# Attention logits of two query blocks made together, the low part of q against the high part of k in two row halves of the array

## The chip, the cores and the metric

The kernel runs on one core of a Trainium2 chip. The metric is the device time of one execution in microseconds (us); the time before is the median of three runs. The profile is of one further execution of the same program.

## What is computed

The reference is a two-layer encoder trunk over 2048 frames of 1024 features. Layer 0 mixes by causal pooling, layer 1 by stick-breaking attention over 16 heads of 64 features. Around them stand projections, norms and gates. The part that matters here is the attention:

```python
logits = jnp.einsum('bhtd,bhsd->bhts', q[:, :, t0:L], k[:, :, :L]).astype(jnp.float32) * SB_SCALE
...
log_keep = jnp.where(mask, jax.nn.log_sigmoid(-logits), 0.0)
later = lax.cumsum(log_keep, axis=log_keep.ndim - 1, reverse=True) - log_keep
log_a = jax.nn.log_sigmoid(logits) + later
a = jnp.where(mask, jnp.exp(log_a), 0.0)
outs.append(jnp.einsum('bhts,bhsd->bhtd', a.astype(v.dtype), v[:, :, :L]))
```

All of it is asked for in float32. The kernel multiplies in the type float32r and carries each operand as a high part and a low part, the low one being what rounding left over; a product is then a sum of several matmuls of parts.

## The kernel before, in words

**Tiling.** The sequence is cut into four chunks of 512 frames (`W5`), and each chunk into four blocks of 128. Features lie on the 128 partitions. The dense layers of a chunk are written as a generator, `stream()`, which yields after each matmul. They compute q, k and v per chunk and write the parts of q and k to memory outside the core as `qd` and `kd`: for each head two layers (high, low) of 64 features by 512 frames.

**Attention.** The list `slots` holds one entry per query chunk, head and key chunk: 160 in all, namely 16 heads times 1, 2, 3 and 4 key chunks. Each slot has four steps, one for each block `j` of 128 queries. In the slot where key chunk and query chunk are the same (`diag`), block `j` needs only the first `(j + 1) * 128` keys, so its width is 128, 256, 384 or 512; in all other slots it is 512. A step does, in the order in which it is written out:

- `turn` (L750) transposes pieces of the finished weights of five steps ago (`LAG_T`) through TensorE into a `psa` bank; ScalarE copies the high part out (L758), VectorE takes the low part (L760, written later in the step).
- at `j == 0`, `begin(i + 1)` (L799) issues the loads of the next slot: `load_k` (L711), and for a new head `load_q` (L704). At `j == 3`, `begin_v` (L810) loads v.
- `front` (L730) makes the logits of block `j` in a `psl` bank with two matmuls, and a sigmoid by ScalarE (L739) takes them out to a tile `pp`.
- the scan of the step before (L743, VectorE) multiplies along the keys.
- `fill` (L844) takes about half of the step's share of dense matmuls (`psd` banks) from the stream.
- `gather` (L762) multiplies transposed weights of seven steps ago (`LAG_G`) by v into a `pso` bank, and `fill` follows again.

**Order.** While attention runs, `state["hold"]` is set, and TensorE's instructions keep the order in which the program writes them (L46 and L50 are the two helpers through which all go). Loads of q, k, v and dense weights (`wpair`, L156) are all issued on the queue of SyncE (SP), one after the other. There are eight PSUM banks, two for each of the tags `psl`, `psa`, `pso` and `psd`.

**The operands of the logits.** For a head, `kk` holds 128 partitions: the high part of k on 0 to 63 and the low part on 64 to 127. `qa` holds the high part of q above the low part, `qb` the same with the halves exchanged. The first matmul sums high by high and low by low over the 128 partitions, the second low by high and high by low. Two buffers serve `kk` (L103), four serve `qa` and `qb` together (L105). At the very beginning, `load_first` (L342) borrows buffers of these tags for the first eight tiles of the input.

Of the kernel before, what the change touches and what calls it, by code (L numbers as in the profile page):

```python
# [9 lines left out]
F32 = mybir.dt.float32  # L10
F32R = mybir.dt.float32r
# [4 lines left out]
P = 128  # L16
# [4 lines left out]
HD = 64  # L21
W5 = 512
# [9 lines left out]
def f(ap):  # L32
    return ap.bitcast(F32)
# [3 lines left out]
def trunk_kernel(ctx, tc, x, p, a_norm, wu_t, wz_a, w_group, a_scale, a_w_out, kv_norm, w_kv,  # L37
                 k_norm, b_norm, b_w_q, b_w_z, b_q_norm, b_w_out, ple_a, ple_b, gate_a, gate_b, out):
    nc = tc.nc
# [15 lines left out]
    cp = ctx.enter_context(tc.tile_pool(name="cp", bufs=1))  # L55
# [19 lines left out]
    g_s, g_b, g_kv = (gains[:, i * KT : (i + 1) * KT] for i in range(3))  # L75
    gqk = cp.tile([P, 1], F32, name="gqk")
    gs = cp.tile([P, 2], F32, name="gs")
    halo = [[cp.tile([P, HALO], F32, name=f"halo{o}_{i}") for i in range(2)] for o in range(KT)]
    for o in range(KT):
        V.memset(halo[o][0], 0.0)  # L80

    def scratch(name, shape):
        return dram.tile(shape, F32, name=name)
# [4 lines left out]
    qd = [[scratch(f"qd{s}_{h}", [2, HD, W5]) for h in range(NH)] for s in range(NSUB)]  # L88
    kd = [[scratch(f"kd{s}_{h}", [2, HD, W5]) for h in range(NH)] for s in range(NSUB)]
# [3 lines left out]
    pool = ctx.enter_context(tc.tile_pool(name="pool", bufs=2))  # L93
    psum = ctx.enter_context(tc.tile_pool(name="psum", bufs=2, space=bass.MemoryType.PSUM))

    def flat(tag, bufs, dt=F32):
        return lambda nm, dt=dt: pool.tile([P, W5], dt, tag=tag, name=nm, bufs=bufs)
# [4 lines left out]
    row = flat("row", 6)  # L102
    keyt = flat("kk", 2, F32R)  # L103
    valt = flat("vv", 3, F32R)
    qryt = flat("q", 4, F32R)  # L105
    ppt = flat("pp", 9)
    pair = lambda nm: pool.tile([P, 2, W5], F32R, tag="act", name=nm, bufs=16)
    t4 = lambda nm: pool.tile([P, 2, W5], F32R, tag="t4", name=nm, bufs=3)
# [2 lines left out]
    def bank(tag, nm):  # L111
        return psum.tile([P, W5], F32, tag=tag, name=nm)
# [227 lines left out]
    first_x = []  # L340

    def load_first():  # L342
        for o in range(KT):
            xin = (qryt, ppt, keyt, valt)[(0, 2, 0, 3, 0, 2, 0, 3)[o]]("xin", F32)
            (nc.sync, nc.scalar)[o % 2].dma_start(out=xin, in_=x[o * P : (o + 1) * P, 0:W5])
            first_x.append(xin)

# [354 lines left out]


    def load_q(c, h):  # L704
        qa, qb = qryt("qa"), qryt("qb")
        nc.sync.dma_start(out=f(qa), in_=qd[c][h].rearrange("l d n -> (l d) n"))
        for l in range(2):
            nc.sync.dma_start(out=f(qb)[(1 - l) * HD : (2 - l) * HD], in_=qd[c][h][l])
        return qa, qb

    def load_k(kc, h):  # L711
        kk = keyt("kk")
        nc.sync.dma_start(out=f(kk), in_=kd[kc][h].rearrange("l d n -> (l d) n"))
        return kk

    def load_v(kc, h):
        vv = valt("vv").rearrange("q (k n) -> q k n", k=4)
# [3 lines left out]
    def load_ends(c, b):  # L721
        en = pool.tile([P, 4, 4], F32, tag="en", name="en")
        for j in range(4):
            nc.sync.dma_start(out=en[:, :, j], in_=ve[c][b][j].rearrange("(m q) -> q m", q=P))
        return en

    last = {}
    ends = {}

    def front(st, j):  # L730
        w = (j + 1) * P if st["diag"] else W5
        r0 = W5 - w
        ps = bank("psl", "psl")
        qs = slice(j * P, (j + 1) * P)
        (qa, qb), kk = st["q"], st["k"]
        T.matmul(ps[:, :w], qa[:, qs], kk[:, :w], start=True, stop=False)
        T.matmul(ps[:, :w], qb[:, qs], kk[:, :w], start=False, stop=True)
        pp = ppt("pp")
        A.activation(out=pp[:, r0:], in_=ps[:, :w], func=AF.Sigmoid, scale=-1.0)  # L739

        def scan():
            least = floor[:, r0:][:, ::-1] if st["diag"] else floor[:, 0:1].to_broadcast([P, w])
            V.tensor_tensor_scan(out=pp[:, r0:][:, ::-1], data0=pp[:, r0:][:, ::-1], data1=least,  # L743
                                 initial=1.0 if st["diag"] else st["carry"][j], op0=ALU.mult, op1=ALU.max)
            st["carry"][j] = pp[:, r0 : r0 + 1]
            st["a"].append((pp, r0))

        return scan

    def turn(st, kt):  # L750
        j0 = kt if st["diag"] else 0
        pt = bank("psa", "psa")
        for j in range(j0, 4):
            pp, r0 = st["a"][j]
            T.transpose(pt[:, j * P : (j + 1) * P], pp[:, r0 + kt * P : r0 + (kt + 1) * P], ident)
        at = att("at")
        cs = slice(j0 * P, W5)
        A.copy(out=at[:, 0, cs], in_=pt[:, cs])  # L758
        st["at"][kt] = at
        return lambda: V.tensor_tensor(out=at[:, 1, cs], in0=pt[:, cs], in1=f(at[:, 0, cs]), op=ALU.subtract)  # L760

    def gather(st, kt):  # L762
        cs = slice((kt if st["diag"] else 0) * P, W5)
        if st["diag"] and kt == 0:
            st["o"].append(bank("pso", "pso"))
        po, at, vv = st["o"][0], st["at"].pop(kt), st["v"]
        T.matmul(po[:, cs], vv[:, kt, :], at[:, 0, cs], start=(st["diag"] and kt == 0), stop=False)
        T.matmul(po[:, cs], vv[:, kt, :], at[:, 1, cs], start=False, stop=(st["last"] and kt == 3))
        if st["last"] and kt == 3:
            half, os, c, h2 = st["h"] % 2, st["os"], st["c"], st["h"] // 2  # L770
            mine, other = slice(half * HD, (half + 1) * HD), slice((1 - half) * HD, (2 - half) * HD)
            A.copy(out=os[mine], in_=po[other])
            V.tensor_tensor(out=os[mine], in0=po[mine], in1=os[mine], op=ALU.add)  # L773
            if half:
                gated(c, h2, os)
# [16 lines left out]
    active, head = {}, {}  # L792
    run = stream()

    def until(mark):
        while mark not in marks:
            next(run)

    def begin(i):  # L799
        c, h, kc = slots[i]  # L800
        until((c, h // 8))
        if kc == c:
            if h % 8 == 0:
                ends[c, h // 8] = load_ends(c, h // 8)
            os = head["os"] if h % 2 else pool.tile([P, W5], F32, tag="os", name="os", bufs=2)
            head.clear()
            head.update(q=load_q(c, h), carry=[None] * 4, o=[], os=os)
        active[i] = dict(head, c=c, h=h, k=load_k(kc, h), diag=kc == c, last=kc == 0, a=[], at={})

    def begin_v(i):  # L810
        c, h, kc = slots[i]
        active[i]["v"] = load_v(kc, h)

    def rate(i):
        c = slots[min(i, len(slots) - 1)][0]
        parts = 66 + (0, 0, -8, 8)[c]
        return (parts * 24.0) / (64 * (c + 1) - (5 if c < NSUB - 1 else 0))

    nc.scalar.dma_start(out=g_a, in_=a_norm)
    pump()  # L820
    fold_load(3)
    load_first()
    wq["by"] = nc.sync
    wq["cap"] = UNITS
# [10 lines left out]
    until((0, 0))  # L835
    state["solo"], state["hold"] = False, True
    begin(0)
    begin_v(0)
    for _ in range(60):
# [4 lines left out]
    def fill(share):  # L844
        nonlocal owed, count
        owed += share
        while owed >= 1.0:
            next(run, None)
            owed -= 1.0
            count += 1  # L850
            if count % 36 == 0 and kept and (1, 0) in marks:
                keep(*kept.pop(0))

    scan = None
    for n in range(4 * len(slots) + LAG_G):
        i, j = divmod(n, 4)
        x_ = rate(i)
        i2, j2 = divmod(n - LAG_T, 4)
        low = turn(active[i2], j2) if 0 <= i2 < len(slots) else None
        due, scan = scan, None  # L860
        if i < len(slots):
            if j == 0 and i + 1 < len(slots):
                begin(i + 1)
            if j == 3 and i + 1 < len(slots):
                begin_v(i + 1)
            scan = front(active[i], j)
        if due:
            due()
        if low:
            low()  # L870
        fill(x_ / 2)
        i3, j3 = divmod(n - LAG_G, 4)
        if 0 <= i3 < len(slots):
            gather(active[i3], j3)
            if j3 == 3:
                active.pop(i3)
        fill(x_ / 2)
# [69 lines left out]
```

## Time and profile before

| | |
|---|---|
| time, median of 3 runs | 2834.18 us (2833.43 to 2836.98) |
| time of the profiled execution | 2834.65 us |
| its span, first to last instruction | 2832.9 us |
| matmuls | 13400 |
| of these for logits (`psl`) | 1280 |
| bytes moved by DMA | 643.37 MB |
| mean granted clock of TensorE | 0.985 |

The span is nearly all of the time. Lines of the profile name an engine (PE is TensorE's matmuls, PEld its weight loads, DVE is VectorE, ACT ScalarE, POOL GpSimd, SP SyncE and SPq its DMA queue), the source line, the operation, the tiles as out<-in, and the shape. In a group the count follows an x, then come the busy time, the mean duration of one in ns, and the idle time ahead of it with what ended it. In a timeline the first number is the start in us from the beginning of the span, the second the time until the last of the merged instructions ends. In the table by stages, the first number after the bounds is the length, followed by the busy time and count of each engine, the granted clock, the share of the DMA engines and GB/s.

### The profile page before, as it was taken

How to read it: one execution, taken by the hardware profiler on the slowest of the kernel's cores; microseconds unless marked ns; L12 is line 12 of the kernel's file. 1: busy time of each engine (PE TensorE's matmuls, PEld its weight loads, DVE VectorE, ACT ScalarE, POOL GpSimd, SP SyncE). 2: the span in 40 equal slices, each digit the busy share in tenths (PEclk: the TensorE clock that was granted, in tenths of full speed). 3: DMA queues.
4: the chain of work that ended last, by engine and by line, in shares of the span. 5: the costliest groups of instructions: out<-in, count | busy, mean ns of one | idle time of the engine just before them, and what ended most of it. 6: DMA issues, size and time to landing. Idle time of an engine off the chain costs nothing.

```text
span 2832.9 us, 38130 instructions
## 1 busy us (share of the span) xinstructions
PE 2733.4 (96%) x13400; PEld 2246.7 (79%) x13400; DVE 1840.4 (65%) x2369; ACT 1271.2 (45%) x2496; POOL 870.4 (31%) x699
## 2 busy tenths in 40 slices
PE   7999979999988999999999999999999999999999
PEld 7888857878866787788778888888888888888777
DVE  5645444655334686766458888776777877777872
ACT  4435542344433445545344456554454444444441
POOL 1354422455423354553213434221211101111002
PEclk8999989999999999999999999999999999999999
DMA  5647899556788966786776444778577667656535
GB/s 213 222 142 278 309 323 307 178 176 208 257 258 282 334 224 218 235 308 228 244 251 219 146 147 153 241 225 274 177 230 240 244 213 255 207 198 230 176 127 185
DMA packets 306123, 643.37 MB, mean 227 GB/s; under 512 B 48646, under 2 KB 81414, under 8 KB 305932
## 3 DMA queue, kind: packets, MB, share of 16 engines
q1 hardware_dynamic: 304348, 639.62, 68.1%
q8 instruction: 105, 1.72, 0.3%
q10 hardware_dynamic: 1584, 1.33, 0.1%
q14 instruction: 86, 0.70, 0.1%
HBM read 471.43 MB, written 161.02 MB: 223 GB/s over the span
## 4 chain that ended last, share of the span: by engine, by line
PE 79%; DMA 8%; DVE 5%; SPq 2%; issue 2%; ACT 2%; POOL 2%; ACTq 0%; DVEq 0%; POOLq 0%
PE psd L46 55%; PE psl L46 8%; PE pso L46 7%; PE psa L50 7%; DMA wpair<-once 3%; DVE pp L743 2%; DVE at L760 1%; DMA wraw<-in_b_w_q_dram 1%; PE pst L50 1%; DMA xin<-in_x_dram 1%; DMA vs<-vr 1%; POOL wpair L144 1%; PE pst L46 1%; SPq L523 1%; DMA kraw<-in_b_w_out_dram 1%
## 5 line engine op out<-in xcount | busy, mean ns | idle before, releaser
L743 DVE TENSOR_TENSOR_SCAN pp<-pp,floor 128x512 f32<-128x512 f32 (+3 forms) x640 | 774.7, 1210 | 34.5 <-ACT pp L739 33.6
L760 DVE TENSOR_TENSOR at<-psa,at 128x512 fp32r<-128x512 f32 (+3 forms) x640 | 387.1, 605 | 431.9 <-ACT at L758 429.6
L46 PE MATMUL psd<-wpair,x 128*128 128x512 f32 x2304 | 620.5, 403 | 38.8 <-DMA wpair<-once 22.7
L758 ACT CAST at<-psa 128x512 fp32r<-128x512 f32 (+3 forms) x640 | 333.6, 521 | 690.6 <-PE psa L50 665.4
L46 PE MATMUL psd<-x,wpair 128*128 128x512 f32 x2304 | 599.3, 393 | 3.5 <-ACT sg L481 3.5
L46 PEld LDWEIGHTS psd<-wpair,x 128*128 128x128 f32 x2304 | 426.0, 191 | 139.6 <-DMA wpair<-once 38.0
L46 PEld LDWEIGHTS psd<-x,wpair 128*128 128x128 f32 x2304 | 427.0, 188 | 92.5 <-ACT sg L481 4.6
L46 PE MATMUL psd<-xp,wpair 128*128 128x512 f32 x1536 | 391.8, 396 | 6.4 <-DMA wpair<-once 6.4
L50 PE MATMUL psa<-ident,pp 128*128 128x128 f32 x2176 | 347.2, 274 | 17.4 <-DVE pp L743 6.6
L46 PE MATMUL pso<-at,vv 128*128 128x512 f32 (+3 forms) x1280 | 361.5, 364 | 0.2 <-DVE at L760 0.2
L50 PEld LDWEIGHTS psa<-ident,pp 128*128 128x128 f32 x2176 | 274.8, 141 | 104.8 <-DVE at L760 12.2
L739 ACT ACTIVATE pp<-psl 128x512 f32<-128x512 f32 (+3 forms) x640 | 344.6, 538 | 12.5 <-PE psl L46 9.2
L46 PEld LDWEIGHTS psd<-xp,wpair 128*128 128x128 f32 x1536 | 287.4, 190 | 66.3 <-DMA wpair<-once 7.7
L46 PE MATMUL psl<-kk,qa 128*128 128x512 f32 (+3 forms) x640 | 284.4, 444 | 2.9 <-DMA kk<-kd 2.9
L46 PEld LDWEIGHTS pso<-at,vv 128*128 128x128 f32 x1280 | 240.7, 189 | 54.0 <-DVE at L760 0.5
L46 PE MATMUL psl<-kk,qb 128*128 128x512 f32 (+3 forms) x640 | 234.2, 366 | 0.0
L46 PE MATMUL psd<-og,wpair 128*128 128x512 f32 x744 | 202.6, 395 | 2.0 <-DVE os L773 2.0
L46 PE MATMUL psd<-mp,wpair 128*128 128x512 f32 x768 | 196.9, 398 | 7.5 <-DVE xr L449 7.5
L144 POOL TENSOR_TENSOR wpair<-wraw,wpair 128x512 fp32r<-128x512 f32 x101 | 148.4, 1474 | 128.3 <-ACT wpair L142 127.9
L46 PEld LDWEIGHTS psd<-mp,wpair 128*128 128x128 f32 x768 | 145.0, 192 | 38.2 <-DVE xr L449 8.3
L46 PEld LDWEIGHTS psd<-og,wpair 128*128 128x128 f32 x744 | 137.5, 188 | 31.5 <-DVE os L773 2.6
L474 POOL TENSOR_TENSOR xj<-x 128x512 f32<-128x512 f32 x64 | 101.7, 1594 | 135.5 <-DVE sg L485 129.6
(112 smaller groups left out, 2747.4 us busy)
## 6 DMA issues: line engine op xcount, KB each, us to landing
wpair<-once SPq DMA_DIRECT2D x384, 512.0 KB
once<-wpair SPq DMA_DIRECT2D x80, 512.0 KB
kk<-kd SPq DMA_DIRECT2D x160, 256.0 KB
vv<-vd SPq DMA_DIRECT2D x160, 256.0 KB
wpair<-wf SPq DMA_DIRECT2D x48, 512.0 KB
once<-kp SPq DMA_DIRECT2D x36, 512.0 KB
wraw<-in_a_w_out_dram SPq DMA_DIRECT2D x64, 256.0 KB
wraw<-in_gate_a_dram SPq DMA_DIRECT2D x64, 256.0 KB
```

The costliest lines, as they stand in the source:

```text
L46: return held_in_order(nc.tensor.matmul(*a, **k))
L50: return held_in_order(nc.tensor.transpose(*a, **k))
L144: (G if state["lo"] % 3 else V).tensor_tensor(out=pr[:, 1], in0=raw, in1=f(pr[:, 0]), op=ALU.subtract)
L474: G.tensor_tensor(out=xj, in0=f(x1[o][:, 0]), in1=f(x1[o][:, 1]), op=ALU.add)
L523: nc.sync.dma_start(out=vs[lo + 1 : hi + 1], in_=vr[lo:hi])
L739: A.activation(out=pp[:, r0:], in_=ps[:, :w], func=AF.Sigmoid, scale=-1.0)
L743: V.tensor_tensor_scan(out=pp[:, r0:][:, ::-1], data0=pp[:, r0:][:, ::-1], data1=least, initial=1.0 if st["diag"] else st["carry"][j], op0 ...
L758: A.copy(out=at[:, 0, cs], in_=pt[:, cs])
L760: return lambda: V.tensor_tensor(out=at[:, 1, cs], in0=pt[:, cs], in1=f(at[:, 0, cs]), op=ALU.subtract)
```

## The change

`front` now makes two blocks at once, in steps 0 and 2 of a slot. `qa` holds the high part of q twice, on both halves of the partitions, so that a whole-array matmul with `kk` gives high by high and high by low. What is left is the low part of q by the high part of k, over 64 features: for the first block it is multiplied on partitions 0 to 63, for the second on 64 to 127, each into its own bank. The product of the two low parts is no longer made. For the second operand, the high part of k must lie on both halves: in even slots `kk` has it on the lower-numbered half and the extra tile `key2` on the other, in odd slots `kk` is loaded with its halves exchanged and `key2` is filled on the first. `qb` becomes a tile of 2 by 128 columns, which holds the low parts of blocks 0 and 2 on one half and of 1 and 3 on the other. The scans are kept in a queue, one per step as before. `load_first` takes two tiles of the tag `at` in place of four of `q`.

```diff
+    key2 = cp.tile([P, W5], F32R, name="key2")
...
-    qryt = flat("q", 4, F32R)
+    qryt = flat("q", 2, F32R)
...
     def load_first():
+        two = [pool.tile([P, 2, W5], F32, tag="at", name="xin", bufs=3) for _ in range(2)]
         for o in range(KT):
-            xin = (qryt, ppt, keyt, valt)[(0, 2, 0, 3, 0, 2, 0, 3)[o]]("xin", F32)
+            xin = (keyt, valt)[o // 2 % 2]("xin", F32) if o % 2 else two[o // 4][:, o // 2 % 2]
...
     def load_q(c, h):
-        qa, qb = qryt("qa"), qryt("qb")
-        nc.sync.dma_start(out=f(qa), in_=qd[c][h].rearrange("l d n -> (l d) n"))
-        for l in range(2):
-            nc.sync.dma_start(out=f(qb)[(1 - l) * HD : (2 - l) * HD], in_=qd[c][h][l])
+        qa = qryt("qa")
+        qb = pool.tile([P, 2, P], F32R, tag="qb", name="qb", bufs=2)
+        low = qd[c][h][1].rearrange("d (a e n) -> e d a n", a=2, e=2)
+        for e in range(2):
+            nc.sync.dma_start(out=f(qa)[e * HD : (e + 1) * HD], in_=qd[c][h][0])
+        for e in range(2):
+            nc.sync.dma_start(out=f(qb)[e * HD : (e + 1) * HD], in_=low[e])
         return qa, qb
 
-    def load_k(kc, h):
+    def load_k(kc, h, turn):
         kk = keyt("kk")
-        nc.sync.dma_start(out=f(kk), in_=kd[kc][h].rearrange("l d n -> (l d) n"))
-        return kk
+        if turn:
+            for l in range(2):
+                nc.sync.dma_start(out=f(kk)[(1 - l) * HD : (2 - l) * HD], in_=kd[kc][h][l])
+        else:
+            nc.sync.dma_start(out=f(kk), in_=kd[kc][h].rearrange("l d n -> (l d) n"))
+        other = slice((1 - turn) * HD, (2 - turn) * HD)
+        nc.sync.dma_start(out=f(key2)[other], in_=kd[kc][h][0])
+        return [key2, kk] if turn else [kk, key2]
...
-    def front(st, j):
-        w = (j + 1) * P if st["diag"] else W5
+    def front(st, j0):
+        js = (j0, j0 + 1)
+        (qa, qb), high, full = st["q"], st["k"], st["k"][st["turn"]]
+        banks = [bank("psl", "psl") for _ in js]
+        widths = [(j + 1) * P if st["diag"] else W5 for j in js]
+        for j, ps, w in zip(js, banks, widths):
+            T.matmul(ps[:, :w], qa[:, j * P : (j + 1) * P], full[:, :w], start=True, stop=False)
+        for e, ps, w in zip(range(2), banks, widths):
+            half = slice(e * HD, (e + 1) * HD)
+            T.matmul(ps[:, :w], qb[half, j0 // 2], high[e][half, :w], start=False, stop=True)
+        return [ran(st, j, ps, w) for j, ps, w in zip(js, banks, widths)]
+
+    def ran(st, j, ps, w):
         r0 = W5 - w
-        ps = bank("psl", "psl")
-        qs = slice(j * P, (j + 1) * P)
-        (qa, qb), kk = st["q"], st["k"]
-        T.matmul(ps[:, :w], qa[:, qs], kk[:, :w], start=True, stop=False)
-        T.matmul(ps[:, :w], qb[:, qs], kk[:, :w], start=False, stop=True)
         pp = ppt("pp")
...
-        due, scan = scan, None
+        due = scans.popleft() if scans else None
...
-            scan = front(active[i], j)
+            if j % 2 == 0:
+                scans.extend(front(active[i], j))
```

More of the change, by code (lines that the diff above doesn't have):

```diff
@@ L807, in begin @@
             head.update(q=load_q(c, h), carry=[None] * 4, o=[], os=os)
-        active[i] = dict(head, c=c, h=h, k=load_k(kc, h), diag=kc == c, last=kc == 0, a=[], at={})
+        active[i] = dict(head, c=c, h=h, turn=i % 2, k=load_k(kc, h, i % 2), diag=kc == c, last=kc == 0, a=[], at={})
     def begin_v(i):
@@ L852, in fill @@
                 keep(*kept.pop(0))
-    scan = None
+    scans = deque()
     for n in range(4 * len(slots) + LAG_G):
```

## The prediction

> **What bounds the kernel now.** I read the page's busy times and chain first, to learn which engine sets the end, then the table by stages, to see where that holds.
>
> ```profile
> span 2832.9 us, 38130 instructions
> PE 2733.4 (96%) x13400; PEld 2246.7 (79%) x13400; DVE 1840.4 (65%) x2369; ACT 1271.2 (45%) x2496; POOL 870.4 (31%) x699
> PE 79%; DMA 8%; DVE 5%; SPq 2%; issue 2%; ACT 2%; POOL 2%; ACTq 0%; DVEq 0%; POOLq 0%
> ```
>
> TensorE is busy 96% of the span and holds 79% of the chain. The span is 2832.9 us; the profiled execution took 2834.65 us, 0.5 us above the median of the three runs, 2834.18.
>
> ```profile
> core 0: us, PE busy (x) PEld busy (x) DVE busy (x) ACT busy (x) POOL busy (x), PEclk, DMA share, GB/s
> 385.00:600.00 215.00, 200.81 (x910) 163.18 (x911) 120.34 (x161) 76.12 (x146) 73.49 (x66) 0.95 0.75 250
> 600.00:1000.00 400.00, 377.88 (x1786) 305.94 (x1785) 196.78 (x266) 162.13 (x328) 160.38 (x132) 0.98 0.78 261
> 1000.00:1500.00 500.00, 482.57 (x2367) 393.12 (x2367) 325.27 (x397) 241.06 (x485) 209.96 (x161) 0.99 0.75 246
> 1500.00:2000.00 500.00, 496.25 (x2536) 410.90 (x2535) 400.47 (x485) 254.39 (x508) 153.72 (x116) 1.00 0.62 197
> 2000.00:2500.00 500.00, 497.71 (x2551) 412.07 (x2551) 372.49 (x447) 230.82 (x453) 77.13 (x57) 1.00 0.68 223
> 2500.00:2735.00 235.00, 227.92 (x1179) 185.50 (x1178) 188.67 (x225) 115.61 (x229) 23.59 (x16) 0.99 0.57 189
> ```
>
> The attention steps lie between 385 and 2735 us. PE idles 14.2 + 22.1 us of the first 615 us there (6%), 3.5% of the next 500, then 0.8%, 0.5% and 3.0%. So array time removed from the steps comes off the span nearly whole. The next engine, VectorE, is busy 80% of its fullest stretches (400.47 of 500, 188.67 of 235) and has room for a few per cent.
>
> **What one logits matmul costs.** A matmul's duration is no price, since matmuls overlap; its price is the distance from its start to the next start. The timeline of one head's diagonal block, TensorE alone, shows it for the narrow widths, a second stretch for the full width.
>
> ```profile
> 1501.15 0.31 PE L46 MATMUL psl<-kk,qa 128*128 128x128 f32 x1
> 1501.29 0.27 PE L46 MATMUL psl<-kk,qb 128*128 128x128 f32 x1
> 1501.40 1.14 PE L46 MATMUL psd<-xp,wpair 128*128 128x512 f32 x4
> ...
> 1504.34 0.28 PE L46 MATMUL psl<-kk,qb 128*128 128x256 f32 x1
> 1504.46 1.09 PE L46 MATMUL psd<-xp,wpair 128*128 128x512 f32 x4
> ...
> 1507.14 0.34 PE L46 MATMUL psl<-kk,qb 128*128 128x384 f32 x1
> 1507.32 1.09 PE L46 MATMUL psd<-xp,wpair 128*128 128x512 f32 x4
> ```
>
> ```profile
> 1529.26 1.09 PE L46 MATMUL psd<-xp,wpair 128*128 128x512 f32 x4
> 1529.96 0.58 PEld L50 LDWEIGHTS psa<-ident,pp 128*128 128x128 f32 x4
> 1530.19 0.60 PE L50 MATMUL psa<-ident,pp 128*128 128x128 f32 x4
> 1530.52 0.19 PEld L46 LDWEIGHTS psl<-kk,qa 128*128 128x128 f32 x1
> 1530.54 0.47 PE L46 MATMUL psl<-kk,qa 128*128 128x512 f32 x1
> 1530.63 0.19 PEld L46 LDWEIGHTS psl<-kk,qb 128*128 128x128 f32 x1
> 1530.86 0.39 PE L46 MATMUL psl<-kk,qb 128*128 128x512 f32 x1
> 1530.86 0.88 PEld L46 LDWEIGHTS psd<-xp,wpair 128*128 128x128 f32 x4
> 1531.08 1.09 PE L46 MATMUL psd<-xp,wpair 128*128 128x512 f32 x4
> ```
>
> The second logits matmul costs 0.11 us at 128 columns, 0.12 at 256, 0.18 at 384 and 0.22 to 0.23 at 512 (four dense ones take 1529.26 to 1530.19, 0.93, so 0.2325 each; I take 0.23). Three more readings of these rows are needed below. Weight loads follow each other at 0.11 us (1530.52, 1530.63), which is the floor that the 128-column matmul shows. A load starts when the matmul before its own begins to stream: one load ahead, no more. And the change from transposes to matmuls costs nothing: from the first transpose (1530.19) to the second logits matmul (1530.86) pass 0.67 us, which is four times 0.11 plus 0.23.
>
> **The change part by part.** Before, each of the 640 steps has two whole-array matmuls. After, two steps share four: two whole ones, then two with 64 rows of weights each, one in the upper and one in the lower half of the array, into different banks. The instruction count is the same; what goes is the time of one matmul per pair, if the halves stream together.
>
> ```profile
> L46 PE MATMUL psl<-kk,qb 128*128 128x512 f32 x448 | 176.5, 394 | 0.0
> L46 PE MATMUL psl<-kk,qb 128*128 128x384 f32 x64 | 21.6, 337 | 0.0
> L46 PE MATMUL psl<-kk,qb 128*128 128x256 f32 x64 | 18.5, 289 | 0.0
> L46 PE MATMUL psl<-kk,qb 128*128 128x128 f32 x64 | 17.6, 275 | 0.0
> ```
>
> (1) The pairs. A diagonal slot has one step of each width, so there are 64 of them, with 64 of the 448 full steps; the other 384 are in slots off the diagonal and make 192 pairs of 512 and 512. Each saves 0.23: 44.2 us. In a diagonal slot the pair 384 with 512 saves the narrower, 0.18: 64 x 0.18 = 11.5 us. The pair 128 with 256 takes 0.11 + 0.12 now, and two weight loads at 0.11 take as long: nothing. Sum 55.7 us, the most there is; the least is zero, if the halves run one after the other.
>
> (2) The second half's weights. To start beside the first half they must be loaded two loads ahead, which no row shows. Both loads fit under the whole matmul before (2 x 0.11 = 0.22 against 0.23), and the lower rows' place is free then. If the load waits until the first half streams, each pair loses 0.11: 192 x (0.23 - 0.11) + 64 x (0.18 - 0.11) = 27.5 us are saved instead of 55.7. I take the first.
>
> (3) Changing between whole array and halves, 640 times. Not in this trace: every matmul is 128*128. The nearest row is the change from transposes to matmuls, about 0. The upper end: the array empties at each change. A 512 matmul is given as 0.394 long and costs 0.23, so a tail of 0.164 is hidden now; exposed twice per pair that is 320 x 0.328 = 105 us, and with a weight load of 0.11 exposed as well each time 175 us. I take 0.02 us, near the transposes and what readings of 0.01 us leave open: 13 us.
>
> The page TensorEngine Tiling (Array Packing) of the Trainium skill, section Tiling Modes, says that changing the tiling mode drains the array, while the tiles of one mode work in parallel. Transposes do not count as such a mode there, so this trace neither confirms nor denies it; by it the sum would be that of the slower rival below. The page TensorE: Matmul & The Clock Gate, Part 3, gives starts about 4 ns apart for matmuls in different row groups, which speaks for (1) and (2); no run here shows it yet.
>
> (4) ScalarE and the banks. A pair takes both `psl` banks at once, so both sigmoids must be done before the next pair, two steps on.
>
> ```profile
> L739 ACT ACTIVATE pp<-psl 128x512 f32<-128x512 f32 x448 | 269.8, 602 | 6.9 <-PE psl L46 3.6
> L758 ACT CAST at<-psa 128x512 fp32r<-128x512 f32 x448 | 262.6, 586 | 539.5 <-PE psa L50 525.5 <-PE psl L46 13.0
> ```
>
> Two sigmoids and a cast are 1.8 us; the steps above stand some 3 us apart (1501.29, 1504.34 and 1507.14 are the same matmul of successive ones), so two steps give 6. Cost zero; without that cover a pair would wait the 0.6 us of a sigmoid. The scan of each step keeps its place, and its sigmoid is earlier or as early.
>
> (5) The loads, all on SP's queue.
>
> ```profile
> L706 SPq DMA_DIRECT2D qa<-qd x64: 319/320/1361, 346.3 to 2677.1; - x64
> L708 SPq DMA_DIRECT2D qb<-qd x128: 450/582/1652, 348.8 to 2678.4; - x128
> ...
> L713 SPq DMA_DIRECT2D kk<-kd x160: 318/326/1834, 380.0 to 2718.2; - x160
> ```
> ```profile
> SPq L156 <- PE psd L46: 380.6, 226, 12.3
> SPq L718 <- PE pso L46: 240.0, 79, 10.1
> ```
>
> Per head q goes from one whole and two half issues to four halves; per slot k gains one half in even slots, and goes from one whole to three halves in odd ones. At 0.58 and 0.32 us: q 64 x (4 - 2) x 0.58 - 64 x 0.32 = 54 us, k 80 x 0.58 + 80 x (3 x 0.58 - 0.32) = 160 us, 214 us of queue time over 2350. It lies beside TensorE: the queue already stands 380.6 + 240.0 us waiting for TensorE to give back weight and value buffers, and k is asked for four steps before its use. Bytes: k 160 x 128 KB more, q 64 x 128 KB less, 12.6 MB on 643, 2%. I cost this at 1 us. Its upper end goes by the one wait for keys in the trace:
>
> ```profile
> L46 PE MATMUL psl<-kk,qa 128*128 128x128 f32 x64 | 19.4, 304 | 2.9 <-DMA kk<-kd 2.9
> ```
>
> 2.9 us in each of the 16 slots of the first query block, which load q and k every slot, is 46.
>
> (6) `key2` is written for the next slot while this slot reads its other half: no wait if halves are kept apart by the program's waits. `load_first` uses other fresh buffers for the same eight loads: zero.
>
> **Sum.** 55.7 - 13 - 1 = 41.7, less 3% for the stretches in which TensorE idles anyway: 40.4 us. 2834.65 - 40.4 = 2794.2, by the median run 2793.8. I predict 2794.
>
> **The rivals.** (a) Late second load: the halves start 0.11 apart; 27.5 - 13 - 1 = 13.5 us saved, 2821. For it speaks that a load starts only one matmul ahead in the rows above. (b) The halves run one after the other: no saving, and 0 to 13 us of changes, 2835 to 2848. (c) Slower: the array empties at each change. 105 us paid against 55.7 saved is 2834.65 + 49 = 2884; with the exposed load, 2834.65 + 119 = 2954. It decides from 55.7 / 640 = 0.087 us per change, about half the hidden tail. Against it stands the free change out of transposes; for it, that nothing here shows a change of the rows in use, and that a sum passing through 128 rows must leave before 64-row sums can go another way. The skill's draining rule above is this mechanism. (d) Loads late in the first block: up to 46 us back, 2839.
>
> **Chances.** The forecast 0.44 (with changes from 0 to 0.04 us each: 2778 to 2808); (a) 0.14; (b) 0.09; (c) 0.29, of which 0.12 beyond 2884; (d) 0.04. Within 0.2% means 5.7 us, about what a measurement of this kernel can tell from no change. (a), and the forecast, are faster: 0.58. Same: (d) and half of (b), some 0.09. Slower: (c) and the rest, 0.33. The range goes from 2778 (all 55.7 us) to 2884 (the empty array with its loads hidden); 0.12 lie above and a few per cent below.
>
> **What would show it.** Right: in the timeline the second half's start stands under 0.05 us behind the first's, and the next matmul 0.23 behind both; `psl` matmuls' share of the chain falls from the present by a quarter. Rival (a): 0.11 between the halves. (b): 0.23. (c): a gap above 0.23 between the second whole matmul and the first half, and between the halves and the next dense matmul; PE's sum of gaps grows. (d): TensorE waiting for `kk`, `key2` or `wpair` loads. I would be wrong first of all by (3), the one price that no row of this trace carries.

## The result, and the profile after

The changed kernel takes 2924.32 us (median of four runs, 2920.57 to 2926.54) against 2834.18 us: 1.0315 times as long, 95% interval 1.0297 to 1.0333. It is 90 us slower. The profiled execution took 2926.54 us, its span is 2924.8 us.

The page of the changed kernel, its busy times and, from the costliest groups, the half matmuls:

```profile
span 2924.8 us, 38785 instructions
PE 2806.3 (96%) x13400; PEld 2188.3 (75%) x13400; DVE 1851.9 (63%) x2369; ACT 1283.1 (44%) x2496; POOL 850.6 (29%) x699
...
L46 PE MATMUL psl<-key,qb 64*128 64x256 f32 (+2 forms) x320 | 151.3, 473 | 1.3 <-DMA key<-kd 1.3
L46 PE MATMUL psl<-kk,qb 64*128 64x128 f32 (+2 forms) x320 | 147.2, 460 | 0.0
```

There are as many matmuls as before, 640 of them on 64 rows, and TensorE is again busy for 96% of a longer span. Busy time can't tell running from standing here, since a matmul's end is modelled. The starts can. This is TensorE's timeline of one pair off the diagonal, first the matmuls, then the weight loads of the same stretch:

```profile
1802.19 0.60 PE L50 MATMUL psa<-ident,pp 128*128 128x128 f32 x4
1802.55 0.72 PE L46 MATMUL psl<-kk,qa 128*128 128x512 f32 x2
1803.19 0.50 PE L46 MATMUL psl<-key,qb 64*128 64x512 f32 x1
1803.19 0.50 PE L46 MATMUL psl<-kk,qb 64*128 64x512 f32 x1
1803.62 1.21 PE L46 MATMUL psd<-x,wpair 128*128 128x512 f32 x4
1804.67 0.33 PE L46 MATMUL pso<-at,vv 128*128 128x128 f32 x2
```

```profile
1802.52 0.30 PEld L46 LDWEIGHTS psl<-kk,qa 128*128 128x128 f32 x2
1803.19 0.18 PEld L46 LDWEIGHTS psl<-key,qb 64*128 64x128 f32 x1 [0.37 <-issue]
1803.19 0.18 PEld L46 LDWEIGHTS psl<-kk,qb 64*128 64x128 f32 x1
1803.62 0.53 PEld L46 LDWEIGHTS psd<-x,wpair 128*128 128x128 f32 x3 [0.25 <-issue]
```

The two halves start in the same hundredth of a microsecond, 1803.19: they do stream together. (Lines with the operand `key` read the tile `key2`.) But from the first transpose to the `pso` matmul pass 1804.67 - 1802.19 = 2.48 us, where four transposes (0.44), two whole matmuls (0.46), one matmul's time for the halves (0.23) and four dense ones (0.93) make 2.06. So 0.42 us are lost on each visit to the halves, and at most 0.23 saved. The weight loads show how. Before, each load started while the matmul ahead of its own was streaming. Now the loads of the halves start only at 1803.19, as late as the half matmuls themselves, and the next whole array's load only at 1803.62. Half of 0.42 us is 0.21 for each change: a weight load of 0.11 us stands in the open, and the other 0.1 us is what is left over. It fits an array that first runs empty, which no row shows by itself. The stretch is typical: over all 192 visits off the diagonal the halves start a median of 0.33 us after the second whole matmul, and the next whole one 0.43 us after them.

### The profile page after: what moved, and what is told of

The parts are those of the page before. It is cut to its first block, busy times and chain, and to the rows that moved or that the text cites. A ratio compares the mean times of both kernels' runs of the same rounds, so it can differ in the third digit from the quotient of the medians.

```text
span 2924.8 us, 38785 instructions
## 1 busy us (share of the span) xinstructions
PE 2806.3 (96%) x13400; PEld 2188.3 (75%) x13400; DVE 1851.9 (63%) x2369; ACT 1283.1 (44%) x2496; POOL 850.6 (29%) x699
## 4 chain that ended last, share of the span: by engine, by line
PE 59%; DVE 5%; DMA 4%; ACT 1%; issue 1%; SPq 1%; POOL 1%; ACTq 0%; DVEq 0%; POOLq 0%
PE psd L46 37%; PE psl L46 7%; PE pso L46 7%; PE psa L50 7%; DVE pp L760 3%; DMA wpair<-once 3%; DVE at L777 1%; PE pst L50 1%; DMA kk<-kd 0%; DMA wraw<-in_gate_a_dram 0%; ACT pp L756 0%; DVE os L790 0%; SPq L525 0%; POOL wpair L145 0%; DMA vs<-vr 0%
## 5 line engine op out<-in xcount | busy, mean ns | idle before, releaser
L760 DVE TENSOR_TENSOR_SCAN pp<-pp,floor 128x512 f32<-128x512 f32 (+3 forms) x640 | 758.2, 1223 | 54.2 <-ACT pp L756 52.6
L46 PE MATMUL psd<-wpair,x 128*128 128x512 f32 x2304 | 640.4, 413 | 45.4 <-DMA wpair<-once 28.3
L46 PE MATMUL psd<-x,wpair 128*128 128x512 f32 x2304 | 615.6, 400 | 3.0 <-ACT sg L483 1.9
L46 PEld LDWEIGHTS psd<-x,wpair 128*128 128x128 f32 x2304 | 416.1, 188 | 100.7 <-issue 17.8
L46 PE MATMUL psd<-xp,wpair 128*128 128x512 f32 x1536 | 400.3, 402 | 4.5 <-DMA wpair<-once 4.5
L756 ACT ACTIVATE pp<-psl 128x512 f32<-128x512 f32 (+3 forms) x640 | 307.9, 533 | 77.0 <-PE psl L46 74.9
L46 PE MATMUL psl<-kk,qa 128*128 128x512 f32 (+3 forms) x640 | 210.0, 410 | 7.8 <-DMA kk<-kd 7.8
L46 PE MATMUL psd<-og,wpair 128*128 128x512 f32 x744 | 210.7, 405 | 2.4 <-DVE os L790 2.4
L46 PE MATMUL psl<-key,qb 64*128 64x256 f32 (+2 forms) x320 | 151.3, 473 | 1.3 <-DMA key<-kd 1.3
L46 PE MATMUL psl<-kk,qb 64*128 64x128 f32 (+2 forms) x320 | 147.2, 460 | 0.0
```

The costliest lines, as they stand in the source:

```text
L46: return held_in_order(nc.tensor.matmul(*a, **k))
```

## The experiments

Theory A after the result: the visits to the halves cost the time. Rivals: B, the order of two blocks at once and the added loads cost it; C, the halves stream slowly. In the diffs the changed kernel is the starting point where nothing else is said. All times are medians; the kernel before, run beside them, had medians of 2835.2 to 2837.1 us.

### e1_whole_low: no halves

```diff
-            T.matmul(ps[:, :w], qb[half, j0 // 2], high[e][half, :w], start=False, stop=True)
+            T.matmul(ps[:, :w], qb[:, j0 // 2], full[:, :w], start=False, stop=True)
```

> The changed kernel, but the low part is multiplied by two whole-array matmuls in place of the two half ones; order and loads stay. (It leaves out the right low product: both blocks get the sum of both blocks' low parts.) Theory A: each visit to the halves costs about 0.41 us beyond streaming (the array runs empty at both changes, and the next weights load only after that), against at most 0.23 us saved; without the visits that is 192 x 0.17 + 64 x 0.21 + 64 x 0.28 = 64 us less than the changed kernel, about 2860, and the 26 us above the kernel before that remain are waits for later loads. Rival B: the loss is the order of two blocks at once and the extra loads, and the halves are free: 2924 + 55 = 2979, as two whole matmuls take longer than two halves together. Rival C: the halves stream slowly (0.43 us a pair): also near 2860, not told apart here.

Measured 2918.94 us (1.0253 to 1.0300 times before), against A's 2860 and B's 2979. Without a single visit the time hardly fell. The waits of SP's queue show that this kernel has a wait of its own:

```profile
SPq L724 <- DMA key<-kd: 190.2, 94, 5.3
```

The queue stands 190.2 us until an earlier load of `key2` has landed. Nothing reads `key2` any more, and the program's list of SP's instructions has these three in a row (in brackets the semaphores that a load waits for; when it lands, the first signals DMAHW6 and the second DMAHW7):

```
715 L724 DMA key2_109<-kd1_5_315 64x512 [waits DMAHW6_49,DMAHW2_49]
716 L724 DMA key2_109<-kd1_6_316 64x512 [waits DMAHW7_49,DMAHW6_49]
717 L724 DMA key2_109<-kd1_7_317 64x512 [waits DMAHW7_49,DMAHW0_49]
```

The second waits for the first and the third for the second, and all three write the same half of `key2`. Loads into different halves do not wait for each other: in the same list the 16 loads from `kd0` for the second query chunk, into the lower half, all stand ahead of the first load from `kd1` for that chunk, into the other half, although the two alternate in the written order. Without a reader nothing spaces the loads of a half out. They run far ahead of the logits, one directly behind the other, and each stands at the head of SP's queue until the one before it has landed. Their rows, e1 first and the changed kernel below, show it (durations of the shortest, median and longest in ns, then the starts of the first and the last in us):

```profile
L724 SPq DMA_DIRECT2D key<-kd x160: 444/451/3576, 379.6 to 2261.1; - x160
L724 SPq DMA_DIRECT2D key<-kd x160: 444/461/1386, 383.6 to 2808.3; - x160
```

In the changed kernel a reader stands between two loads of a half, so e1 tells nothing on the visits; the next runs had to.

### e2_one_k_load and e10_halves_one_k_load: the same without key2, without and with visits

```diff
-        other = slice((1 - turn) * HD, (2 - turn) * HD)
-        nc.sync.dma_start(out=f(key2)[other], in_=kd[kc][h][0])
-        return [key2, kk] if turn else [kk, key2]
+        return [kk]
...
-        active[i] = dict(head, c=c, h=h, turn=i % 2, k=load_k(kc, h, i % 2), diag=kc == c, last=kc == 0, a=[], at={})
+        active[i] = dict(head, c=c, h=h, turn=0, k=load_k(kc, h, 0), diag=kc == c, last=kc == 0, a=[], at={})
```

e2 has this and e1's edit; e10 has this and, for the low part:

```diff
+            T.matmul(ps[:, :w], qb[half, j0 // 2], full[half, :w], start=False, stop=True)
```

> As e1_whole_low, but k is loaded by one issue per slot as before the change, without key2. (The same product is left wrong.) If the 26 us of waits come from the loads of k: about 2836. If they come from the loads of q or from making two blocks at once: about 2860, as e1_whole_low.

> e2_one_k_load with the visits put back: half matmuls of 64 rows in both row halves, but both read kk, so that k is loaded by one issue and there is no key2. (The second block of each pair is multiplied with the low part of k instead of the high one.) Theory: 320 visits cost 65 us by the starts in the changed kernel's trace, so 2859 + 65 = 2924, the changed kernel's own time, and the three issues of k and key2 cost it nothing. Rival: the issues of k cost part of it, as e1 and e9 suggest: then 2924 less that part, and at least 2870.

e2: 2859.07 us (1.0052 to 1.0089). e10: 2910.61 us (1.0248 to 1.0283). The only difference between them is the visits, and they cost 51.5 us. The sum by starts was 65. Some of it is covered, as e2's TensorE stands more for other engines, for instance 14.5 us for VectorE's copy out of the transposes' bank, and with the visits such a wait is shorter (this one accounts for 4 of the 13 us):

```profile
PE psa L50 <- DVE at L774: 14.5, 16, 2.7
```

```profile
PE psa L50 <- DVE at L774: 10.1, 14, 2.5
```

(the first row from the waits of e2, the second from those of e10). What is left is 23 us from e2 to the kernel before, and 14 from e10 to the changed one.

### e3_halves_twice and e5_two_visits: more streaming in a visit, more visits

```diff
+        for stop in (False, True):
+            for e, ps, w in zip(range(2), banks, widths):
+                half = slice(e * HD, (e + 1) * HD)
+                T.matmul(ps[:, :w], qb[half, j0 // 2], high[e][half, :w], start=False, stop=stop)
```

> The changed kernel with each pair of half matmuls issued twice in a row. (The low product is counted twice.) Theory A: a second pair inside one visit changes nothing of the layout and costs only its streaming: 0.23 us in 256 visits and 0.11 to 0.23 in 64, 66 to 74 us, about 2990 to 3000. Rival C (halves stream slowly): 0.43 in each, 320 x 0.4 = 128 us or more, 3050. If the second pair's weights can't be loaded ahead either: 0.11 more in each, 35 us on top of the first, 3030.

e5, in the place of the two loops:

```diff
+        for e, j, ps, w in zip(range(2), js, banks, widths):
+            half = slice(e * HD, (e + 1) * HD)
+            T.matmul(ps[:, :w], qa[:, j * P : (j + 1) * P], full[:, :w], start=True, stop=False)
+            T.matmul(ps[:, :w], qb[half, j0 // 2], high[e][half, :w], start=False, stop=True)
```

> The changed kernel with the order whole, half, whole, half: each half matmul is a visit of its own, 640 in place of 320, and none beside another. Theory A: 320 more visits at 0.41 = 131 us, and the 55 us saved by streaming together are lost: 2924 + 186 = 3110. Rival B (changes are free): 2924 + 55 = 2979. Rival C (a pair of halves is slow because two tiles share something): 2950 or less, as a half alone is then no dearer than a whole matmul.

e3 took 2977.69 us, 53 more than the changed kernel, where A said 66 to 74 and C 128 or more; a second pair inside a visit adds no more than its streaming, so the halves are not slow. Nor is it half loads as such that can't run ahead. These are TensorE's weight loads in one visit of e3, off the diagonal, whose first pair of matmuls starts at 1841.82:

```profile
1841.82 0.18 PEld L46 LDWEIGHTS psl<-key,qb 64*128 64x128 f32 x1 [0.36 <-issue]
1841.82 0.18 PEld L46 LDWEIGHTS psl<-kk,qb 64*128 64x128 f32 x1
1841.92 0.19 PEld L46 LDWEIGHTS psl<-key,qb 64*128 64x128 f32 x1
1841.93 0.19 PEld L46 LDWEIGHTS psl<-kk,qb 64*128 64x128 f32 x1
1842.48 0.53 PEld L46 LDWEIGHTS psd<-x,wpair 128*128 128x128 f32 x3 [0.36 <-issue]
```

The second pair's weights are loaded 0.10 us behind the first pair's start, under its matmuls; only the loads on either side of a change of rows wait.

e5 took 3064.01 us, 140 more, where A said 186, B 55 and C 26 or less; why it is 46 less than A said is not traced. Both are single runs, and the distances are far beyond the few us by which such runs differ. TensorE's timeline of e5, one pair on the diagonal:

```profile
1856.17 0.30 PE L46 MATMUL psl<-kk,qa 128*128 128x128 f32 x1
1856.40 0.33 PE L46 MATMUL psl<-kk,qb 64*128 64x128 f32 x1
1856.66 0.38 PE L46 MATMUL psl<-kk,qa 128*128 128x256 f32 x1
1856.97 0.38 PE L46 MATMUL psl<-key,qb 64*128 64x256 f32 x1
1857.28 0.98 PE L46 MATMUL psd<-x,wpair 128*128 128x512 f32 x3
```

From the 128-column half (1856.40) to the next whole matmul (1856.66) pass 0.26 us, where a 128-column matmul cost 0.11 at this place before the change; from the 256-column whole one to its half, and from there to the dense one, 0.31 each, where 256 columns cost 0.12. At 512 columns both distances are 0.42 us (medians of 448), where a matmul takes 0.23: 0.38 more in a visit, near the 0.42 of a pair. So a half alone is about as dear at its two changes as a pair, and the price goes with the change of rows in use, not with two halves at once. B and C fall as explanations of the main part.

### e6_off_diagonal: fewer visits

```diff
+            if st["diag"]:
+                T.matmul(ps[:, :w], qb[:, j0 // 2], full[:, :w], start=False, stop=True)
+            else:
+                T.matmul(ps[:, :w], qb[half, j0 // 2], high[e][half, :w], start=False, stop=True)
```

> The changed kernel with halves only in slots off the diagonal: 192 visits of 320 stay; in diagonal slots the low part goes through two whole matmuls. (There the low product is left wrong, as in e1.) By the starts in the changed kernel's trace a diagonal visit costs 0.21 us (384 with 512) or 0.28 (128 with 256) more than it saves: 64 x 0.21 + 64 x 0.28 = 32 us less, 2892. If the visits were not what costs: 2924 or more.

2906.66 us, 18 less than the changed kernel in place of 32. The direction is A's. The kernel also has slots in which nothing reads `key2`, and with them a part of e1's wait (81.0 us in SP's queue), so the size tells little.

### e9_key2_read: a miss

e1 with a one-column copy of `key2` by ScalarE after each slot's second pair, to give the tile a reader.

> e1_whole_low again, but with key2 read by a one-column ScalarE copy at the end of each slot's logits, so that its next load waits for a reader, as in the changed kernel, and not for the landing of the load before it (in e1 SP stood 190 us for that). If that wait made e1 slow: near e2_one_k_load, 2859 to 2870, which leaves the visits to the halves some 60 us of the changed kernel's 90. If the three issues of k per slot cost as much as e1 says: 2919 again.

2942.49 us, slower than e1. The copy turned into a wait itself:

```profile
ACT seen L756 <- DMA key<-kd: 275.6, 132, 8.4
```

Each copy waits for the load of its own half, and the next load into that half waits for the copy. Nothing ties this chain to the logits, so it still runs ahead, to a last copy at 2277.7 us of 2933.8, and its waits now stand in ScalarE's queue too. This prices nothing.

### e19_halves_two_k: the number of issues

e10 with k loaded by two half issues per slot.

```diff
+        for l in range(2):
+            nc.sync.dma_start(out=f(kk)[l * HD : (l + 1) * HD], in_=kd[kc][h][l])
```

> e10_halves_one_k_load with k loaded by two half issues per slot in place of one whole one: 160 more issues, the same bytes, no key2. (The second block is multiplied with the low part of k, as in e10.) If the number of issues makes the 14 us between e10 (2911) and the changed kernel (2924): about 2918 to 2924. If key2, whose loads wait for readers of the whole tile, makes them: 2911.

2919.30 us (1.0271 to 1.0309): 8.7 of the 14 us come with 160 more issues and no more bytes. The medians of e10 and e19 were measured beside different runs of the kernel before, 1 us apart, and the intervals of their ratios touch (1.0248 to 1.0283 and 1.0271 to 1.0309), so the 8.7 is rough. The 5 us that remain to the changed kernel are not clear of noise. The other theory counted on readers of the whole tile; as said under e1, the waits keep the two halves apart.

### e7_pairs_old_loads and e8_single_new_q: two blocks at once

e7 is the kernel before with `front` called for two blocks in the even steps, and four whole matmuls; e8 is the kernel before with the changed loads of q.

```diff
+        for qt, first in ((qa, True), (qb, False)):
+            for j, ps, w in zip(js, banks, widths):
+                T.matmul(ps[:, :w], qt[:, j * P : (j + 1) * P], kk[:, :w], start=first, stop=not first)
```

> The kernel before with one thing of the change: logits of two blocks are made in steps 0 and 2 (four whole-array matmuls, full result, loads of q and k as before). If making two blocks at once is what cost the 23 us of e2_one_k_load: about 2859. If the four half loads of q cost them: about 2836.

> The kernel before, one block per step, with the changed loads of q (four half issues, and load_first on other buffers); the second matmul is a whole-array one over the new low tile. (The low product is left wrong: each block gets the sum of two blocks' low parts.) The mirror image of e7: about 2836 if two blocks at once cost the 23 us, about 2859 if the loads of q do.

e7: 2861.02 us (1.0073 to 1.0100). e8: 2838.30 us (0.9996 to 1.0015). Making two blocks at once costs 24 to 25 us by itself (2861.02 against 2836.37 beside it), the loads of q nothing that can be measured. Set side by side by their dense and `pso` matmuls, e7 is 22 us behind the kernel before when that stands at 1436 us, and 26 at the end: nearly all of it is lost while the dense layers of the first chunks run beside attention. These are the sums from 385 us to that point, the kernel before first:

```profile
sum 1051.00, PE 1000.95 PEld 814.27 DVE 605.02 ACT 451.08 POOL 430.91; mean PE 111.22 PEld 90.47 DVE 67.22 ACT 50.12 POOL 47.88
sum 1073.00, PE 1009.42 PEld 820.21 DVE 609.74 ACT 452.82 POOL 420.41; mean PE 112.16 PEld 91.13 DVE 67.75 ACT 50.31 POOL 46.71
```

Of the 22 us, 13.5 are idle time of TensorE (63.6 in place of 50.1). The other 8.5 are longer busy time for the same matmuls, and the granted clock of the stretch is 0.97 in place of 0.98.

### e11, e12, e13: why two blocks at once cost

Three single edits on e7. e11 writes `begin` in step 1. e12 writes the second sigmoid a step later. e13 shares out the dense matmuls:

```diff
-        fill(x_ / 2)
+        fill((x_ + (2 if j % 2 else -2)) / 2)
```

> e7_pairs_old_loads with the next slot's loads of q and k written one step later (step 1 in place of 0), after the pair that precedes them. Theory P1: making two blocks at once costs 24 us because the loads of q and k then stand earlier in SP's queue and hold up others while they wait for TensorE (184 + 124 us of such waits against 62 + 54 before): 2836 to 2845. Theory P2 (bunched work on ScalarE and VectorE): 2860, as e7.

> e7_pairs_old_loads with the second block's sigmoid written one step later, so that ScalarE gets one per step as before the change; the four matmuls stay together. Theory P2: two sigmoids in a row delay the copy out of the transposes' bank and the work of the dense layers, so this brings back most of the 24 us: 2836 to 2845. Theory P1: 2860.

> e7_pairs_old_loads with the dense matmuls shared out so that all steps are equally long on TensorE again: two fewer in the even steps, which have four logits matmuls, and two more in the odd ones, which have none. e11 and e12 did not bring the 24 us back. Theory P3: the steps of unequal length cost them, because TensorE reaches the next step's transposes and dense results before VectorE and ScalarE are done with the last: 2836 to 2845. If neither queue order nor step length is the cause: 2860 again, and what it is stays open.

2863.00, 2863.14 and 2860.10 us: none moved it. Two theories fell, the loads' place in the queue and steps of unequal length. e12 did not test its own: its trace has the second sigmoid directly behind the first and the second scan behind the first, as e7's has, because only TensorE is held to the written order. In both traces 298 of the 320 pairs of scans run directly one behind the other, in the kernel before none. VectorE's timeline of e7, with TensorE's row that waited:

```profile
1088.20 2.01 DVE L747 TENSOR_TENSOR_SCAN pp<-pp,floor 128x128 f32<-128x128 f32 x2
1090.13 0.66 DVE L449 TENSOR_TENSOR xr<-psd,xr 128x512 f32<-128x512 f32 x1
...
1090.85 1.65 PE L46 MATMUL psd<-mp,wpair 128*128 128x512 f32 x3 [7.81 <-DVE xr L449]
```

Two scans (x2) take 2.01 us in a row, ahead of the addition that empties a dense bank, for which TensorE stood idle 7.81 us, the longest of its waits in this run. The scans fill only the end of that wait; before them VectorE had other work and stood for ScalarE. All of TensorE's waits for this addition, the kernel before first, then e7:

```profile
PE psd L46 <- DVE xr L449: 7.5, 2, 4.2
PE psd L46 <- DVE xr L449: 11.3, 2, 7.8
```

So this wait accounts for at most 4 of the 24 us.

### e14 to e18: holding the order

e14 holds sigmoids, scans and the two operations on the transposes' bank to the written order, in e12; e15 does so in the changed kernel. e16 and e17 turn the order on VectorE to the one that the kernel before really has, low part first and then the scan of the same step. e18 is e7 with only VectorE held so.

```diff
+            tc.keep_in_program_order(V.tensor_tensor_scan(out=pp[:, r0:][:, ::-1], data0=pp[:, r0:][:, ::-1], data1=least,
```

> e12_pairs_spread_sigmoid with the sigmoids, the scans and the two operations that take the transposes out of their bank held to the written order on ScalarE and VectorE: one scan, then one low part, in each step. If two scans in a row (2.5 us on VectorE, in front of the low part that frees the transposes' bank) are what the 24 us come from: 2836 to 2845. If not: 2860 again, and the cause stays open.

> The changed kernel with the same: second sigmoid written a step later, and sigmoids, scans and the transposes' two operations held to the written order. If the parts add up: 2924 - 24 = 2900, of which 52 above the kernel before are the visits and 14 the loads of k. If the two scans in a row are not the cause: 2924.

> e14 with the order turned to that of the kernel before on VectorE: in each step first the low part of the transposes, then the scan of the same step, one per step, and one sigmoid per step. TensorE still makes the logits of two blocks at once. If two scans in a row are what cost the 24 us: 2836 to 2845. If 2860 or more: it is something else in making two blocks at once, and stays open.

> The changed kernel with the same order on VectorE and ScalarE. If the parts add up: 2924 - 24 = 2900. If the two scans in a row are not the cause: 2924 or more.

> e7_pairs_old_loads with only VectorE's scans and low parts held in order (low part first, then one scan in each step); ScalarE is left free, so that both banks are emptied as early as in e7. If two scans in a row are what cost the 24 us: 2836 to 2845. If the order is held at a price, or the scans are not the cause: 2860 or more, and then the cause stays open.

3004.70, 3066.98, 2982.88, 3052.57 and 2916.89 us: all much slower than what they start from. The scans are apart, but new waits took their place. TensorE's longest waits, e16 first, e18 below:

```profile
PE psl L46 <- ACT pp L743: 75.4, 30, 12.7
PE psa L50 <- DVE at L764: 38.6, 16, 12.5
```

```profile
PE psa L50 <- DVE at L764: 61.4, 25, 12.7
```

In e16 a pair waits up to 12.7 us for a sigmoid, which was moved a step later, since it needs both banks. In e18, where the sigmoids stay together, the held order makes the low part late instead. No run takes the scans apart without adding a wait, so the cause of the 24 us stays open; two scans in a row remain the candidate, argued from the rows of e7 alone.

## Why the prediction was wrong

The forecast was 2794 us, 40 faster; it came out 90 slower. By its own steps:

**(1) The pairs stream together: right.** The halves start within 0.01 us of each other. The saving of up to 0.23 us is real: in e3 a second pair in each visit costs 53 us, 0.17 for two matmuls.

**(2) The second half's weights: right in the result, not in the reason.** They are not late, because they load beside the first half's, at 1803.19 both. But neither load runs under the whole matmul before, which (2) had counted on; that belongs to (3).

**(3) The change between whole array and halves: this step failed.** It was taken as 0.02 us, next to the free change out of transposes, and it is 0.21: 0.42 per visit, ten times the term, beyond the deciding point of 0.087 and between the two ends (0.164, and 0.274 with a weight load). The nearest row was not near: a transpose keeps all 128 rows in use. The rival (c) was the right mechanism, with the weight load in the open as in its second price. Its first price, 2884, served as the end of the range; with the load in the open it said 2954, and the result lies between. That is partly chance: 38 of the 90 us come from steps (4) and (5), and the visits alone (51.5 us) would have given 2886, beside the price that had the load hidden. Of its two parts the tail is shorter than 0.164 (about 0.1) and the load is what was said (0.11). In time, e10 against e2, the visits cost 51.5 us net of the saving; with the 55.7 us of (1) given back that is 0.17 us per change, some of the 0.21 being covered by shorter waits. The page TensorEngine Tiling (Array Packing) of the Trainium skill, section Tiling Modes, says that changing the mode drains the array; the timeline of the changed kernel agrees, with 0.42 us per visit.

**(4) ScalarE and the banks: wrong in its result.** The sigmoids were in time, as it said: TensorE stood 0.2 us for them in e7 and not at all in the changed kernel. But two blocks at once cost 24 us (e7), mostly where VectorE and ScalarE also serve many dense results. The step looked at the banks alone and took for granted that scans keep their place; two of them now run in a row. Whether that is what costs the 24 us stays open.

**(5) The loads: mis-sized.** Costed at 1 us; e10 to the changed kernel is 14, some 9 of them by the number of issues (e19). The loads of q cost nothing that can be measured (e8).

**(6) key2: right as far as the runs show.** The program's waits do keep the two halves apart (e1), and TensorE stood 1.3 us for `key2`. What its loads cost is at most the 5 us of the 14 that e19 leaves, which are not clear of noise.

Together: 24 (pairs) + 52 (visits) + 14 (loads of k) = 90. The last two are steps along one row of kernels (e2, e10, the changed one), so the sum had to close; what is independent in it is that e7 and e2 give the same 23 to 25 us for the pairs.

## What to carry to other kernels

Count a change of the rows in use as 0.2 us on TensorE, as here, about half of it an uncovered weight load, and put as much work into a visit as it needs: by these numbers a visit pays from about two full-width pairs (0.46 us saved), of which these banks hold one; no run tried two. Where an engine's order is not held, two results that become ready together may also be worked off together, in front of others (298 of 320 pairs of scans here); ask for whom they stand in the way. And an experiment that takes away the reader of a buffer, or holds an order, adds waits of its own: look at its waits before its time is read.

## What the runs showed of the hardware

The weight loads of two row halves run side by side (both at 1803.19, 0.18 us), where loads of whole arrays follow each other at 0.11 us. A load for another number of rows does not start under the matmul before it: 0.37 us without any load stand ahead of the halves' loads, and 0.25 ahead of the next whole one, while in e3 a second pair's loads start 0.10 us behind the first pair's matmuls, on the same rows. The change between transposes and whole-array matmuls stayed free in the same trace: from the first transpose to the first logits matmul pass 0.36 us (1802.19 to 1802.55), before the change 0.35.
